# Two-layer diffusion trunk on one core: 22 value and gate tiles of layer 1 moved ahead of its attention, 16 of them in pairs of seven products

## The chip, the cores and the metric

The kernel runs on one core of one Trainium2 chip. The metric is the device time of one execution in microseconds (us). PE is TensorE (matmuls), PEld its weight load, DVE VectorE, ACT ScalarE, POOL GpSimd and SP SyncE; the two last issue most of the DMAs.

## What is computed

One inference step of a trunk with two layers. There are 640 tokens (128 of a prompt, 512 latent) of width D = 2048, all in fp32. Each layer is a norm with a learned shift and scale, one input projection, two attention-like branches, a gate, one output projection and a residual:

```python
hp = rms_norm(xp, norm_g[layer]) * (1.0 + sc_p) + sh_p      # hs likewise for the latent tokens
cq, ck, cv, cg, dq, dk, dv, dg = split_cols(h @ w_in, ODD_SPLIT)        # layer 1
o_c = rms_norm(o1 - lam * o2, c_on) * (1.0 - lam_init)      # C: two softmax maps a head, 4 heads, values 256 wide
y_c = o_c.transpose(0, 2, 1, 3).reshape(b, t, C_W) * jax.nn.silu(cg)
y_d = merge_heads(attend(q_d, dk_all, dv_all)) * jax.nn.silu(dg)        # D: 8 query heads on 2 key/value heads
out = jnp.concatenate([y_c, y_d], axis=-1) @ w_out
xp = xp + gt_p * out_p
```

Prompt tokens see prompt tokens alone; latent tokens see 256 cached keys and the 512 latent ones. The normalised keys and the values of the prompt are outputs too. Layer 1's input projection has 6656 columns: 52 tiles of 128 (cq 8, ck 8, cv 8, cg 8, dq 8, dk 2, dv 2, dg 8).

## The kernel before

Everything is kept transposed: 128 features on the partitions, 640 tokens along the free axis, in two halves of 320. An fp32 number is split in a high and a low part (`split`, L212: ACT copies the high part, DVE subtracts to get the low one), and each fp32 product is three matmuls: high by high, high by low, low by high (`proj_q`, L241; L248, L249, L250). h, the normalised input, stays in SBUF as 16 k-tiles, high and low. A **tile** of a projection is 128 columns: 2 halves x 16 k-tiles x 3 = 96 matmuls of 128x320, with weights loaded by SP in quarters of four k-tiles (`load_raw`, L224) and split ahead of use by ACT (`wh`, L213) and DVE (`wl`, L214).

`run_tiles` (L281) works through a list of jobs, each a column and a generator that post-processes the tile. The first three tiles are the **lead**: they go together, k-tile by k-tile, as `make_h` (in layer 1 `h1_maker`, L1217: per k-tile and token group one DVE scaling L1234, one ACT bias and rounding L1236, one DVE low part L1238) delivers h. Tile 4 needs an accumulator that lead tile 0 holds until its job has read it. Thereafter tiles go one by one; after each quarter `slot` (L273) advances the queue `prep` (post-processing of the last tile) and the queue `attn` by one step. Attention is thus a generator whose steps are interleaved by hand with the quarters of projection tiles; one step issues the scores of a block (`scores`, L681: L687 to L689), the softmax (`soft`, L652: maximum on DVE L654, scale L656 and exponential L661 on ACT, sum's reciprocal L667), transposes of an earlier block's weights (L675) and the products with the values. `k_gen` (L540) and `q_gen` (L587) normalise and rotate keys and queries; because there is one place for q0, q1, k0, k1 and v, they call `drain(attn)` before they overwrite it: whatever is left of the attention then runs at once.

In layer 1 each C head has the tiles ck, cq, ck, cq, cv, cv and the next head's two cg; the attention of a head (`diff_gen`, L1269) is queued after its second cv. D has dk, dv, then dq, dq and two dg per pair of query heads (`pair_gen`, L714). All 52 tiles run as plain tiles, 96 matmuls each.

`run_pairs` (L403) is another way to do two tiles at once, as a 2 x 2 block product with **seven products** in place of eight: 7 x 8 k-tiles x 3 = 168 matmuls for a pair in place of 192. The stationary operands are sums of weights (DVE, L434 and next), the moving ones are h's halves or forms of them: `forms` (L1019) makes, for each j of 8, three sums of h's quarter-blocks (320 columns each) and splits them into `T`, and a fourth one, `t1`, that `begin` (L1124) needs. The seven products are named Q1, N5, P6, Q2, P7, Q3, P4 in their order; the block sums overwrite parts of h (`half_of`) and use four places called `room`. Before the change only the output projections use it (`project_out`, L1072): three lead tiles and one more, then six pairs.

Between the layers the residual x is parked in DRAM (`xdram`) and comes back through `x1_back` (L1211), partly in the pairs' buffers w8, sx and T. The gated results y go to DRAM (`save_y`, L793, on POOL's queue) and are read back for the output projection by `y1_maker` (L1376).

Of the kernel before, what the change touches and what calls it, by code (L numbers as in the profile page):

```python
# [50 lines left out]
def trunk_kernel(ctx: ExitStack, tc: tile.TileContext, I: dict, O: dict):  # L51
# [164 lines left out]
    hs = {}  # L216

    def new_h(k):
        t = hpool.tile([P, 2, NT], F32R, tag=f"h{k}", name=f"h{k}")
        hs[k] = t[:, 0, :], t[:, 1, :]  # L220
        return hs[k]
# [39 lines left out]

    def advance(queue, n):
        for g in queue[:n]:
            if next(g, DONE) is DONE:
                queue.remove(g)
# [15 lines left out]
    def run_tiles(jobs, w_ap, make_h, fill=None, rate=0.0, ahead=None, order=(0, 1, 2, 3), before=None,  # L281
                  last=None, by_half=False, trans=[], grace=0, cut=None, summed=None, led=None, freed=None):
# [85 lines left out]
        for i in range(lead, len(jobs)):  # L368
# [34 lines left out]
    def run_pairs(cols, w_ap, mov, room, begin, done, tail):  # L403
# [60 lines left out]
        def after(p, name, ps):  # L464
# [7 lines left out]
            elif name == "Q2":  # L472
                V.tensor_add(q1, ps, q1)
                done(p, 0, 0, q1)
            elif name == "P7":
                A.copy(u3, ps)
                V.tensor_add(n5, u3, n5)
                done(p, 1, 1, n5)
            elif name == "Q3":
                V.tensor_add(u2, ps, u2)  # L480
                done(p, 0, 1, u2)
            else:
                done(p, 1, 0, ps)
# [56 lines left out]
    def k_gen(ap, pp, tag, src, gain, new_out):  # L540
# [33 lines left out]
        drain(attn)  # L574
# [9 lines left out]
        split(hi[:, CTX + NS:CTX + NT], lo[:, CTX + NS:CTX + NT], t)  # L584


    def q_gen(ap, pp, tag, gain, then=None, wait=True):  # L587
# [28 lines left out]
        drain(attn)  # L616
# [10 lines left out]
    def ctx_v(ap, src, hi, lo, w):  # L627
        raw = ap.tile([P, 2, w], F32, tag="ctxv", name="ctxv", bufs=1)
        nc.sync.dma_start(raw, src.rearrange("(c p) d -> p c d", p=P))
        split(hi[:, 0:2, :], lo[:, 0:2, :], raw)  # L630

    def v_gen(ap, pp, src, new_out, w=P, j=0, then=None):
        x = stage(ap, pp)
        yield
        if j == 0:
            drain(attn)
            st["v"] = tuple(ap.tile([P, 7, w], F32R, tag=t, name=t) for t in ("vh", "vl"))
            ctx_v(ap, src, *st["v"], w)
        hi, lo = st["v"]
        cols = slice(j * P, (j + 1) * P)  # L640
# [7 lines left out]
        if then:  # L648
            attn.append(then())
# [64 lines left out]
    def pair_gen(ap, width, k, banded, emit, done, sinks):  # L714

        v = st["v"]
# [25 lines left out]
        def score(u, j):  # L742
            segs, masks, lo, hi, _ = plan(u)
            q = st[f"q{j}"]
# [43 lines left out]
    xdram = [dram.tile([P, NT], F32, name=f"xd{k}") for k in range(KT)]  # L788

# [98 lines left out]
    def k_job(tag, src, gain, new_out):  # L888
        return lambda pp: k_gen(pools["cur"], pp, tag, src, gains[gain], new_out)
# [7 lines left out]
    def y_pair(i):  # L897
        t = pools["cur"].tile([P, 2, NT], F32, tag="y", name="y", bufs=2)
# [12 lines left out]
    def pair_then(width, kk, i, banded, gated):  # L911

        def then():
# [12 lines left out]
            sinks = [(nsink[:, j:j + 1], sink[:, j:j + 1]) if banded else () for j in (i, i + 1)]  # L926
            return pair_gen(pools["cur"], width, st[kk], banded, emit, done, sinks)
        return then

    def late_gate_job(i, load=False):  # L930
        def f(pp):
            ap = pools["cur"]
            if i < 8:
                drain(attn)
            if load and i % 2 == 0:
                y_pair(i)
                for k in (i, i + 1):
                    nc.sync.dma_start(y[k], ydram[k])
# [47 lines left out]
    for i in range(4):  # L986
# [5 lines left out]
        jobs.append((EV["q"] + (h + 1) * P, q_job("q1", "a_q_norm", pair_then(640, "k0", h, True, gated))))  # L992
# [25 lines left out]

    def forms():  # L1019
# [12 lines left out]
        for j in range(8):  # L1032
# [6 lines left out]
            x2, x3, x4 = (x[:, i * HALF:(i + 1) * HALF] for i in range(3))  # L1039
            V.tensor_sub(x3, b22, b12)  # L1040
            V.scalar_tensor_tensor(out=x2, in0=x3, scalar=-1.0, in1=b11, op0=ALU.mult, op1=ALU.subtract)
            V.scalar_tensor_tensor(out=x4, in0=x2, scalar=-1.0, in1=b21, op0=ALU.mult, op1=ALU.subtract)
            V.tensor_sub(d, b11, b12)
            t = big(f"T{j}", dtype=F32R).rearrange("p (s n) -> p s n", s=2)
            split(t[:, 0, :], t[:, 1, :], x)
            T.append(t)
            t1.append(d)
# [24 lines left out]
    def project_out(l, maker, finish, last, tail):  # L1072

        w = W_OUT[l]

        def job(n):
            def f(pp):
                res_load(l, n)
                for i in range(2):
                    res_sum(l, n, pp[i], CS[:1] if i == 0 else CS[1:])  # L1080
                for _ in range(1 + 2 * l):
                    yield
                finish(n)
            return f

        n0 = N_SINGLE[l]
        go_on = run_tiles([(n * P, job(n)) for n in range(3)], w, maker, order=(0, 2, 1, 3))


        quarters = [(n * P, qd) for n in range(3, n0) for qd in range(4)]  # L1090
# [10 lines left out]
        for n in range(3, n0):  # L1101
# [14 lines left out]
            prep.append(job(n)(pp))  # L1116
            advance(prep, 1)
# [12 lines left out]
        def done(p, t, c, src):  # L1130
            n, h = n0 + 2 * p + t, HX[c]
            res_sum(l, n, src, CS[1:] if h else CS[:1], nhgt if t else hgt)
            if n >= KT - 2:
                last(t, h)
            elif n in seen:
# [3 lines left out]
        run_pairs([(n * P, (n + 1) * P) for n in range(n0, KT, 2)], w,  # L1139
                  {"B11": half_of(0, 0), "T1": half_of(0, 1), "B21": half_of(8, 0), "B22": half_of(8, 1),  # L1140
                   "T2": form_of(0), "T3": form_of(1), "T4": form_of(2)}, room, begin, done, tail)
        drain(prep)


    make_y0 = y_maker(("q0h", "q0l", "q1h", "q1l"), NT)

    def y0_maker(k):
        if k < 4:
            return make_y0(k)
        if k == 8:  # L1150
            close("even")
            open_pool("mid")
            st["acc"] = pools["cur"].tile([P, NT], F32, name="acc")
            st["sq"] = pools["cur"].tile([P, NT], F32, name="sq")
# [51 lines left out]
    def x1_tail(name):  # L1206

        for k in (range(0, 4) if name == "Q2" else (4,)):
            x1_back(k, big("w8", bufs=4) if k < 4 else big("sx"))
# [6 lines left out]

    def h1_maker(k, hv):  # L1217
        if k == 0 and hv[0][0] == 0:
            for g in range(3):
                t = big(f"T{g}")  # L1220
                for i in range(3):
                    x1_back(5 + 3 * g + i, t, i)
            for i in (14, 15):
                x1[i] = st["xr", i]
            nc.sync.dma_start(tables, I["k_tables"])
        if len(hv) == 2 or hv[0][0] == 0:
            new_h(k)
            st["ht", k] = big(f"T{4 + k % 4}")[:, 0:NT]
        t = st["ht", k]
# [3 lines left out]
        for sl, c in toks:  # L1233
            V.scalar_tensor_tensor(out=t[:, sl], in0=x1[k][:, sl], scalar=gsc[1][:, k, c:c + 1],  # L1234
# [5 lines left out]
        if k == KT - 1:  # L1240
            close("mid")
            open_pool("odd")
            odd_start()


# [18 lines left out]
    def diff_then(h):  # L1264
        def then():
            return diff_gen(pools["cur"], h, gated.get(2 * h))
        return then

    def diff_gen(ap, h, gt):  # L1269

        v = st["v"]
        t = y_pair(2 * h) if gt is None else gt
# [4 lines left out]
        def score(u, m):  # L1277
            segs, masks, lo, hi, _ = blk_plan(u, False)
            n = hi - lo
            q = st[f"q{m}"]  # L1280
            s = scores(q, u, st[f"k{m}"], segs)
# [36 lines left out]
        def out(u):  # L1318
# [4 lines left out]
            if gt is None:  # L1323
# [21 lines left out]
    gated.clear()  # L1345
    jobs = []
    heads = (3, 0, 1, 2)
    for n, h in enumerate(heads):
        for m in range(2):
            jobs.append((OD["ck"] + (m * 4 + h) * P,  # L1350
# [119 lines left out]
```

## Time and profile before

| quantity | value |
|---|---|
| median of 3 runs | 2316.81 us (2316.61 to 2318.72) |
| profiled execution | 2320.95 us, its span 2319.2 us |
| mean granted TensorE clock in it | 0.997 |
| PE, DVE, ACT, POOL busy | 98%, 64%, 45%, 6% of the span |
| DMA | 321.91 MB, mean 139 GB/s |
| lead of layer 1 | 1141.5 to 1185.6 us |
| rest of layer 1's projection and attention | to about 2101 us |
| output projection 1 | to the end |

The profile is one execution's trace. A row of a group gives the line of the kernel, engine, operation, output and inputs by the program's names, the number of instructions, and behind the bar busy time, the mean duration in ns, and the idle time ahead of them with what ended it. A row of a timeline is start, duration, engine, line and names, in brackets the idle time before. Rows of stretches give start:end, and for each engine its busy time and count.

### The profile page before, as it was taken

The page shows a single profiled execution, that of the slowest core. Times are in us where ns is not written, and L with a number is a line of the kernel's source. Part 1 is how long each engine was busy: PE and PEld are TensorE (multiplying, and loading weights), DVE is VectorE, ACT ScalarE, POOL GpSimd, SP SyncE. Part 2 cuts the span into 40 slices and gives each one's busy share as a digit, 9 for nine tenths or more (in the row PEclk, how much of TensorE's full clock was granted, in tenths as well). Part 3 has the DMA queues.
Part 4 walks back from the last instruction along what each step waited for, and adds up shares of the span by engine and source line. Part 5 has one row for each costly group of instructions (what it writes and reads, how often), then busy time and mean ns, then how long its engine had stood idle before and what let it go on. Part 6 is the DMA issues. An engine that isn't in the chain of part 4 may idle for free.

```text
span 2319.2 us, 41035 instructions
## 1 busy us (share of the span) xinstructions
PE 2282.3 (98%) x16092; PEld 2209.7 (95%) x16092; DVE 1484.3 (64%) x2674; ACT 1035.5 (45%) x2186; POOL 131.4 (6%) x183
## 2 busy tenths in 40 slices
PE   7999999999999999999999999999999999999999
PEld 5889899999999999999999999999999999999999
DVE  4666978779779776887774445454454443457875
ACT  5325652443522222544554444444445554665443
POOL 1000000000000000000000000001000000000101
PEclk9999999999999999999999999999999999999999
DMA  9975546547367564954431221212222212127642
GB/s 320 294 249 160 158 121 214 151 132 218 115 211 222 179 190 129 291 155 127 162 98 58 79 75 55 87 58 77 75 68 65 62 47 81 48 74 263 189 137 61
DMA packets 371553, 321.91 MB, mean 139 GB/s; under 512 B 15762, under 2 KB 333680, under 8 KB 370848
## 3 DMA queue, kind: packets, MB, share of 16 engines
q1 hardware_dynamic: 363360, 288.92, 41.1%
q0 software_dynamic: 7280, 28.20, 3.4%
q8 instruction: 126, 2.06, 0.4%
q10 hardware_dynamic: 720, 2.16, 0.3%
q14 instruction: 67, 0.55, 0.1%
HBM read 290.79 MB, written 28.44 MB: 138 GB/s over the span
## 4 chain that ended last, share of the span: by engine, by line
PE 91%; DVE 3%; DMA 2%; ACT 2%; issue 1%; POOL 1%; SPq 0%; DVEq 0%; POOLq 0%; ACTq 0%
PE pa L248 11%; PE pb L248 10%; PE pb L249 10%; PE pa L249 10%; PE pb L250 10%; PE pa L250 10%; PE pq L499 4%; PE pq L498 4%; PE pq L497 4%; PE T L675 2%; PE S L687 1%; PE S L689 1%; PE S L688 1%; PE T L166 1%; PE T L526 1%; PE T L736 1%
## 5 line engine op out<-in xcount | busy, mean ns | idle before, releaser
L213 ACT ACTIVATE wh<-raw 128x512 fp32r<-128x512 f32 (+1 forms) x504 | 303.6, 604 | 736.2 <-PE pb L249 659.3
L214 DVE TENSOR_TENSOR wl<-raw,wh 128x512 fp32r<-128x512 f32 (+1 forms) x504 | 329.8, 655 | 388.5 <-ACT wh L213 356.2
L248 PE MATMUL pa<-h,wh 128*128 128x320 f32 x1728 | 551.3, 319 | 5.8 <-DVE sum L315 3.8
L249 PE MATMUL pa<-h,wh 128*128 128x320 f32 x1728 | 536.6, 311 | 0.5 <-DVE h L214 0.4
L250 PE MATMUL pa<-h,wl 128*128 128x320 f32 x1728 | 535.4, 310 | 0.0
L248 PE MATMUL pb<-h,wh 128*128 128x320 f32 x1728 | 535.3, 310 | 0.0
L250 PE MATMUL pb<-h,wl 128*128 128x320 f32 x1728 | 535.1, 310 | 0.0
L249 PE MATMUL pb<-h,wh 128*128 128x320 f32 x1728 | 535.0, 310 | 0.0
L248 PEld LDWEIGHTS pa<-h,wh 128*128 128x128 f32 x1728 | 325.4, 188 | 25.2 <-issue 15.5
L249 PEld LDWEIGHTS pa<-h,wh 128*128 128x128 f32 x1728 | 326.1, 189 | 4.5 <-issue 3.3
L250 PEld LDWEIGHTS pa<-h,wl 128*128 128x128 f32 x1728 | 325.1, 188 | 2.1 <-issue 2.1
L249 PEld LDWEIGHTS pb<-h,wh 128*128 128x128 f32 x1728 | 324.7, 188 | 0.9 <-issue 0.8
L248 PEld LDWEIGHTS pb<-h,wh 128*128 128x128 f32 x1728 | 324.6, 188 | 0.7 <-issue 0.4
L250 PEld LDWEIGHTS pb<-h,wl 128*128 128x128 f32 x1728 | 324.7, 188 | 0.4 <-issue 0.4
L191 DVE SCALAR_TENSOR_TENSOR acc<-adaw,sT,acc 128x1024 f32<-128x1024 f32 x240 | 300.0, 1278 | 0.0
L497 PE MATMUL pq<-h,wh 128*128 128x320 f32 x384 | 120.4, 314 | 1.0 <-ACT wh L213 1.0
L499 PE MATMUL pq<-h,wl 128*128 128x320 f32 x384 | 119.6, 311 | 0.8 <-DVE wl L214 0.8
L498 PE MATMUL pq<-h,wh 128*128 128x320 f32 x384 | 119.4, 311 | 0.0
L661 ACT ACTIVATE p<-S,nm,rq 128x768 f32<-128x768 f32 (+3 forms) x120 | 101.0, 842 | 23.1 <-DVE nm L658 20.0
L654 DVE TENSOR_REDUCE nm<-S 128x1 f32<-128x768 f32 (+3 forms) x120 | 91.9, 766 | 24.9 <-PE S L689 24.1
L213 ACT ACTIVATE pth<-T 128x512 fp32r<-128x512 f32 (+1 forms) x132 | 66.3, 532 | 51.5 <-PE T L675 51.0
L498 PE MATMUL pq<-T,wh 128*128 128x320 f32 x288 | 89.0, 309 | 0.0
(306 smaller groups left out, 3497.6 us busy)
## 6 DMA issues: line engine op xcount, KB each, us to landing
adaw<-in_ada_w SPq DMA_DIRECT2D x128, 512.0 KB, 4.3
raw<-in_od_w_in SPq DMA_DIRECT2D x208, 256.0 KB, 2.8
raw<-in_ev_w_in SPq DMA_DIRECT2D x176, 256.0 KB, 3.3
ada<-in_ada_w SPq DMA_DIRECT2D x32, 1024.0 KB, 8.2
yd<-y POOLq DMA_DIRECT2D x34, 320.0 KB, 3.0
yin<-yd SPq DMA_DIRECT2D x32, 320.0 KB, 4.3
w<-yd SPq DMA_DIRECT2D x32, 320.0 KB, 4.2
w<-in_ev_w_out SPq DMA_DIRECT2D x18, 512.0 KB, 4.9
```

What stands on the lines that cost most here:

```text
L191: V.scalar_tensor_tensor(out=acc[c], in0=w, scalar=sT[:, kt, c:c + 1], in1=acc[c], op0=ALU.mult, op1=ALU.add)
L213: A.activation(hi, x, AF.Copy)
L214: V.tensor_sub(lo, x, hi)
L248: PE.matmul(ps, wh[:, i, :], hi[:, sl], start=(j == js[0] if alone else (pos == 0 and j == 0)), stop=False)
L249: PE.matmul(ps, wh[:, i, :], lo[:, sl], start=False, stop=False)
L250: PE.matmul(ps, wl[:, i, :], hi[:, sl], start=False, stop=(j == js[1] - 1 if alone else (pos == 3 and j == 3)))
L497: PE.matmul(ps, wh[:, j, :], hi, start=(new and h == 0 and j == 0), stop=False, **kw)
L498: PE.matmul(ps, wh[:, j, :], lo, start=False, stop=False, **kw)
L499: PE.matmul(ps, wl[:, j, :], hi, start=False, stop=(h == 1 and j == 3), **kw)
L654: V.tensor_reduce(nm, s, axis=AX.X, op=ALU.max, negate=True)
L661: A.activation(p[:, 0:n], s, AF.Exp, scale=rsc, bias=nm, accum_out=l)
L675: PE.transpose(t[:, i * P:(i + 1) * P], p, ident)
```

## The change

The function `project` is what was common in `project_out`: a lead of three tiles, further singles, then pairs. Layer 1 now calls it first, with 22 tiles called FRONT: the gates 10 to 15 as singles (three of them the lead, while h is made), and then sixteen tiles in eight pairs: values 6, 7, gates 0, 1, values 0, 1, gates 2, 3, values 2, 3, gates 4, 5, values 4, 5, values 8, 9 (tiles 8 and up belong to D). Their results go to DRAM (`vdram`, `ydram`) on POOL's queue by way of a three-buffer place (`kept`, `keep_tile`). The pairs need T and t1 of layer 1's h: `forms1` is queued as an attention generator in the lead at k-tile 8 and advances when h of k-tile j+8 exists. `h1_maker` now scales x in place, since forms1 needs the scaled x again. The half of h that the pairs overwrite is saved to `hdram` k-tile by k-tile (eight DMAs on POOL's queue) and loaded back in the tail of the last pair's product P7 (eight more). The rotary tables are loaded after the pairs, not in the lead.

The other 30 tiles follow in a second `run_tiles` with `mid=True`, an extra attention step in the middle of the second quarter of each tile. Order: per C head cq, cq, ck, ck; for D dq, dq, dk, dq, dq per key head; at the end the gates 6 to 9. Queries have two sets of places ("a", "b"), used in turn. `release(tag)` advances only as long as an attention task that uses that place is queued, where `drain(attn)` emptied the queue. Values come back by `v_load` into one buffer (`vraw`); of a C head's two tiles the second is loaded after the first was transposed (`v_kept`). Gates that were done in FRONT are loaded into y's one buffer (`gated_y`; two before) ahead of the attention that multiplies by them; the late gates 6 to 9 load their y instead (`late_gate_job`).

```diff
+    def release(tag):
+        while any(tag in getattr(g, "tags", ()) for g in attn):
+            advance(attn, 1)
...
             for qd in range(4):
-                proj_q(pp, parts[t], qd, qd, HV[:1] if split_last else HV)
+                if mid and qd == 1:
+                    proj_q(pp, parts[t], qd, qd, HV[:1])
+                    advance(attn, 1)
+                    proj_q(pp, parts[t], qd, qd, HV[1:])
...
-        drain(attn)
+        release(tag)
...
+    def v_load(i):
+        t = pools["cur"].tile([P, NT], F32, tag="vraw", name="vraw", bufs=1)
+        nc.sync.dma_start(t, vdram[i])
+        return t
+
+    def v_kept(ap, first, raw, idx, new_out, then):
...
+        for j in range(len(idx)):
+            cols = slice(j * P, (j + 1) * P)
+            v_rows(ap, x, hi, lo, cols, new_out[:, cols])
+            if j + 1 < len(idx):
+                x = v_load(idx[j + 1])
+                yield
+        attn.append(then())
...
-            V.scalar_tensor_tensor(out=t[:, sl], in0=x1[k][:, sl], scalar=gsc[1][:, k, c:c + 1],
+            V.scalar_tensor_tensor(out=t[:, sl], in0=t[:, sl], scalar=gsc[1][:, k, c:c + 1],
...
+        if len(hv) == 2 or hv[0][0] == 1:
+            if k < 8:
+                nc.gpsimd.dma_start(hdram[k], ht[k][:, :, HV[HX[1]][1]])
+            made.add(k)
+        if k == 8:
+            attn.append(forms1())
+
+    def forms1():
...
+        for j, tag in enumerate((3, 4, 5, 6, 7, 1, 2, 0)):
+            while j + 8 not in made:
+                yield
+            for k in (j, j + 8):
+                for sl, c in TOKS:
+                    A.activation(x1[k][:, sl], x1[k][:, sl], AF.Identity, bias=mod[1][:, k, c:c + 1])
...
+            make_form(x, d, b11, b12, b21, b22, big(f"T{tag}", dtype=F32R))
+            yield
...
+    def front_job(n):
+        def f(pp):
+            kept(n)
+            for i, sl in HV:
+                gate_of(st["kept", n][:, sl], pp[i][:, 0:HALF])
+            keep_tile(n)
+        return f
...
+    def front_out(p, t, c, a, b):
+        n = N_FRONT + 2 * p + t
+        dst = st["kept", n][:, HV[HX[c]][1]]
+        if FRONT[n][0] == "g":
+            if b is not None:
+                V.tensor_add(b, a, b)
+            gate_of(dst, a if b is None else b, -1 if t else 1)
...
+    def front_tail(name):
+        if name == "P7":
+            for j in range(8):
+                nc.gpsimd.dma_start(ht[j][:, :, HV[HX[1]][1]], hdram[j])
+
+    project(I["od_w_in"][0], [front_col(*t) for t in FRONT], N_FRONT, h1_maker, front_job, front_begin, front_out,
+            front_tail, by_half=True)
+    nc.gpsimd.dma_start(tables, I["k_tables"])
...
+    def gated_y(i, late=False):
+        t = y_pair(i, 1)
+        if not late:
+            for k in (i, i + 1):
+                nc.sync.dma_start(y[k], ydram[k])
+        return t
...
+    run_tiles(jobs, I["od_w_in"][0], lambda k: odd_start() if k == 8 else None, mid=True)
```

More of the change, by code (lines that the diff above doesn't have):

```diff
@@ L1070, in form_of, with project @@
         return lambda j: (T[j][:, 0, i * HALF:(i + 1) * HALF], T[j][:, 1, i * HALF:(i + 1) * HALF])
[L1072 to L1090, printed above, removed]
+    def project(w, cols, n0, maker, job, begin, out, tail, by_half=False):
+        go_on = run_tiles([(cols[n], job(n)) for n in range(3)], w, maker, order=(0, 2, 1, 3), by_half=by_half)
+        quarters = [(cols[n], qd) for n in range(3, n0) for qd in range(4)]
         raws, parts = [], []
```

287 lines of the change are left out of this document (185 added, 102 removed).

## The prediction, on record before the changed kernel ran

> **What bounds the kernel now.** I read the page first (busy times, chain, DMA issues), then stretches of the trace, then single starts.
>
> ```profile
> span 2319.2 us, 41035 instructions
> PE 2282.3 (98%) x16092; PEld 2209.7 (95%) x16092; DVE 1484.3 (64%) x2674; ACT 1035.5 (45%) x2186; POOL 131.4 (6%) x183
> PE 91%; DVE 3%; DMA 2%; ACT 2%; issue 1%; POOL 1%; SPq 0%; DVEq 0%; POOLq 0%; ACTq 0%
> L498 PE MATMUL pq<-T,wh 128*128 128x320 f32 x288 | 89.0, 309 | 0.0
> ```
>
> TensorE is busy 98% of the span and 91% of the chain that ended last. A matmul removed from a stretch where PE never waits is therefore time removed. But 309 ns is not its price, because matmuls overlap. The price is the spacing of starts in a stretch that is nothing else. Columns below: stretch, its length, busy time (and count) of PE, PEld, DVE, ACT, POOL, then the granted clock, the DMA share and GB/s.
>
> ```profile
> 950.00:1000.00 50.00, 47.64 (x306) 46.25 (x306) 43.69 (x76) 24.79 (x42) 2.16 (x4) 0.97 0.87 263
> 1050.00:1100.00 50.00, 50.00 (x343) 50.00 (x343) 39.12 (x62) 23.44 (x41) 2.16 (x4) 1.00 0.45 133
> 1138.30:1176.80 38.50, 37.06 (x240) 36.24 (x240) 36.12 (x82) 23.67 (x46) 1.10 (x1) 0.96 0.44 147
> 1185.56:1216.00 30.44, 28.66 (x201) 26.43 (x199) 18.73 (x38) 18.61 (x52) 4.87 (x5) 1.00 0.31 90
> 1981.00:2034.00 53.00, 53.00 (x385) 52.24 (x383) 25.41 (x48) 33.65 (x68) 0.00 (x0) 1.00 0.16 46
> 2063.00:2101.00 38.00, 37.98 (x266) 35.54 (x265) 23.23 (x43) 26.82 (x55) 1.48 (x3) 1.00 0.23 72
> ```
>
> The second row is pairs of seven products in layer 0's output projection: 50.00/343 = 145.8 ns per matmul. PE never waits there, with DVE at 78% and ACT at 47%. The first row holds the start of those pairs, the third the lead of layer 1 (its first three tiles, while h is made). There **DVE is busy 36.1 of 38.5 us**: PE is nearly bound by DVE already.
>
> **The change part by part.**
>
> *Removed.* A pair of tiles by seven products is 7 x 8 x 3 = 168 matmuls against 2 x 96 = 192 before. Eight pairs remove 192 matmuls: 192 x 0.1458 = **-28.0 us**. The instruction order of the two kernels bears the count out (192 fewer on TensorE); the second row shows that pairs can run at full rate.
>
> *The lead of layer 1.* New work stands here: forms1 makes, for each of eight j, the sums that the pairs multiply with. As soon as h for k-tile j+8 exists, the form is appended, so it competes with h itself. Prices, from the same work in layer 0's output projection (rows: busy us, mean ns, idle before):
>
> ```profile
> L1040 DVE TENSOR_TENSOR sx<-w,w 128x320 f32<-128x320 f32 x8 | 3.9, 484 | 0.0
> L1042 DVE SCALAR_TENSOR_TENSOR sx<-sx,w 128x320 f32<-128x320 f32 x8 | 3.9, 485 | 0.0
> L1041 DVE SCALAR_TENSOR_TENSOR sx<-sx,w 128x320 f32<-128x320 f32 x8 | 3.9, 486 | 0.0
> L1043 DVE TENSOR_TENSOR tables<-w 128x320 f32<-128x320 f32 x4 | 1.9, 485 | 0.0
> L214 DVE TENSOR_TENSOR T<-sx,T 128x960 fp32r<-128x960 f32 x8 | 9.3, 1157 | 1.0 <-ACT T L213 1.0
> 1174.12 1.01 DVE L1238 SCALAR_TENSOR_TENSOR h<-T,mod,h 128x512 fp32r<-128x512 f32 x2
> 1175.04 1.01 DVE L1234 SCALAR_TENSOR_TENSOR T<-xr,gsc,sf 128x512 f32<-128x512 f32 x2
> 1175.97 0.68 DVE L214 TENSOR_TENSOR wl<-raw,wh 128x512 fp32r<-128x512 f32 x1
> 1176.58 1.01 DVE L1238 SCALAR_TENSOR_TENSOR h<-T,mod,h 128x512 fp32r<-128x512 f32 x2
> 1185.56 0.31 PE L248 MATMUL pa<-h,wh 128*128 128x320 f32 x1
> ```
>
> One form is 4 x 0.485 + 1.157 = 3.10 us of DVE; the timeline rows show that each instruction starts about 0.08 us before the last ended (1174.12 + 1.01 = 1175.13, next start 1175.04), so five of them take 2.7 us. In the order of DVE's instructions four whole forms stand ahead of the last low half of h: 10.8 us. That half ended at 1176.58 + 1.01 = 1177.59. DVE had 38.50 - 36.12 = 2.4 us to spare, so it now ends between 1186.0 and 1188.4. The gate that empties lead tile 0's accumulator then stands behind six more 0.485 us form steps, one 1.16 us split, three weight splits of about 0.65 and one more form step: about 6 us less overlaps, with 0.5 for the gate itself. Tile 4 needs that accumulator, and so starts at 1192.3 to 1194.7 where it started at 1185.56. I take 1193.9: **+8.3 us** (5, if DVE finds the idle time and the order is kinder, to 12, if nothing overlaps). The four later forms lie beside three single tiles, 3 x 96 x 0.146 = 42 us of PE; they are hidden. ACT carries four 320-to-640-wide steps and a 1 us split per form on 24 of 38.5 us: not the bound.
>
> *The clock.* A lead whose PE starves can lose clock as well:
>
> ```profile
> 153.74 0.61 PE L248 MATMUL pa<-h,wh 128*128 128x320 f32 x1 [2.55 <-DVE sum L315]
> 153.80:157.30 3.50, 3.50 (x14) 3.50 (x15) 1.02 (x4) 0.25 (x1) 0.00 (x0) 0.53 0.32 95
> 987.48 0.41 PE L497 MATMUL pq<-h,wh 128*128 128x320 f32 x1 [0.99 <-ACT wh L213]
> 988.70 0.41 PE L499 MATMUL pq<-h,wl 128*128 128x320 f32 x1 [0.66 <-DVE wl L214]
> 990.24 0.47 PE L499 MATMUL pq<-h,wl 128*128 128x320 f32 x1
> ```
>
> After a gap of 2.55 us the granted clock was 0.53 for 3.5 us and 14 matmuls ran where 24 would have: 10 x 0.146 = 1.5 us lost. After gaps of 0.99 and 0.66 us, two microseconds apart, matmuls were again at the slow pace (0.47 against 0.31 us). The starved lead will hold gaps of that kind: I take one such dip, **+1.5 us** (0 to 3: two). The Trainium skill, "TensorE: Matmul & The Clock Gate", section "HAM oscillation — how this bites in real kernels", gives as the rule that only PE idle gaps above some 3.4 us bring the slow clock; by that rule this term would be zero and the sum 1.5 us lower. The rows above speak against it (2.55 us sufficed, and 0.99 with 0.66), so the term stays.
>
> *Start of the pairs.* The same two gaps at 987-989 came from weights that landed late:
>
> ```profile
> 986.01 1.29 DVE L434 TENSOR_TENSOR sx<-w,raw 128x512 f32<-128x512 f32 x2 [1.88 <-DMA w<-in_ev_w_out]
> ```
>
> They cost 1.65 us and a dip of 1.5, 3.2 in all. Here two more singles than in layer 0's projection stand ahead (3 after the lead, not 1), so loads start earlier: **+0.5** (0 to 3.7).
>
> *From the pairs to the other 30 tiles.* New waits: half 0 of h for k below 8, overwritten by the pairs' sums, comes back by eight 320 KB loads on POOL's queue, issued when the last pair's product P7 has ended and two are left. Nearest price:
>
> ```profile
> yd<-y POOLq DMA_DIRECT2D x34, 320.0 KB, 3.0
> w<-xd SPq DMA_DIRECT2D x4, 320.0 KB, 3.0
> y<-yd SPq DMA_DIRECT2D x2, 320.0 KB, 3.6
> w<-yd SPq DMA_DIRECT2D x32, 320.0 KB, 4.2
> ```
>
> Eight issues at about half a microsecond and 3 us to land are about 7 us; two products (2 x 24 x 0.146 = 7.0 us) cover them. Behind them on POOL stands only the load of the rotary tables, needed much later. **+1** (0 to 6, the whole if the cover is gone). Kept tiles are saved from POOL, which has 131 us of work in 2319, and the eight saves of h go the same way during the lead: 0.
>
> *Attention.* It now has 30 tiles to hide behind, not 52, and five steps per tile instead of four (mid=True). A step needs its scores, then this chain:
>
> ```profile
> 1249.61 0.34 PE L689 MATMUL S<-k0h,q0l 128*128 128x384 f32 x1
> 1250.04 0.95 DVE L654 TENSOR_REDUCE nm<-S 128x1 f32<-128x768 f32 x1
> 1251.17 0.29 ACT L656 ACTIVATE nm<-nm,rq 128x1 f32<-128x1 f32 x1
> 1251.50 0.99 ACT L661 ACTIVATE p<-S,nm,rq 128x768 f32<-128x768 f32 x1
> 1253.96 0.34 PE L687 MATMUL S<-k1h,q1h 128*128 128x384 f32 x1
> ```
>
> From the end of the scores (1249.95) to the end of the exponential (1252.49) are 2.5 to 2.7 us; the next scores start 4.0 us after. With a step at every half quarter (12 matmuls, 1.75 us, plus the step's own matmuls) spacings of 2.3 to 2.9 us come about: just the length of the chain. The stretch 2063-2101 above already runs so (one step per half quarter): 266/37.98 = 7.00 matmuls per us against 385/53 = 7.26 in 1981-2034. At the latter rate 266 take 36.6 us, so 1.4 us were lost there. There are eight such attention groups, seven of them new to it; only one in five of their steps is denser for the mid steps, but the chains now meet more weight splits and loads. I take 0.9 each for seven, less the 1.4 that is no longer paid at the end: **+5** (0 to 14: 2 each).
>
> *Values come back from DRAM.* One buffer (vraw): the second tile of a C head is loaded only when the first is transposed. A 320 KB load takes 3.0 to 3.6 us (rows above); 20 matmuls, 2.9 us, stand between. About 0.5 for each of four heads: **+2** (0 to 4).
>
> *Output projection 1.* The last tile's gate (9) now ends its y last, and y9 is needed as the second k-group: gate, save (3.0) and load back (4.2) are about as long as the 10.6 us until then: **+0.5** (0 to 3). Tables loaded later, x1 scaled in place, gate tiles loaded instead of computed in the window: same work elsewhere, 0. The waits of the second lead (1185-1216: 30.44 - 28.66 = 1.8 us) move with it, 0.
>
> Sum: -28.0 + 8.3 + 1.5 + 0.5 + 1 + 5 + 2 + 0.5 = **-9.2 us**. The profiled execution took 2320.95 (span 2319.2), so 2311.8; that execution lies 4.14 above the median 2316.81, so I predict **2307.6**.
>
> **The rivals.**
>
> *Dense attention eats the gain (no change).* At 2 us per group (+14, not +5) the sum is -0.2: 2316.6. For it: the stretch 2063-2101. Against it: that stretch has a step in every half quarter, the new one only every fifth.
>
> *Slower: the chain of a step outlasts its spacing.* Scores, maximum, exponential and weight splits go through DVE and ACT in order. If weight splits (0.68 each) slip between, a step needs 3.1 us where its spacing is 2.3 to 2.9, and PE, in order too, stops at the next scores. With some 96 steps, five in eight at the short spacing: 60 x 0.4 = 24 us, 19 more than I took: 2326.6. It decides from 0.32 us per short step (60 x 0.32 = 19.2, past 2321.4). Against it: ACT is at 27/38 and DVE at 23/38 in 2063-2101, and PE is busy 37.98 of 38.00 there.
>
> *All new waits hidden.* DVE's forms slip into idle time and steps are spaced evenly: -28 + 5 (lead) + 3: 2296.8. Against it: the full DVE of the lead.
>
> *It does not do what it says.* If pairs were no faster than tiles (DVE-bound by their sums), the 28.0 would be missing and the other terms left: 2316.8 + 18.8 = 2335.6. The second row speaks against it, DVE being 78% there, and the sums into the residual that end a pair there give way to gates of a like number of 320-wide steps.
>
> **How the numbers follow.** Forecast (2302 to 2312) 0.55; no change 0.15; slower 0.13; all hidden 0.15; no saving 0.02. Faster than 2312.2 (0.2%, about what a measurement of this kernel can tell from no change): 0.70. Within 0.2%: 0.15. Slower than 2321.4: 0.15. Bounds of the terms, all low: -28 + 5, less 1.4: 2292; all high: far past 2330; two such ends at once are unlikely. The range **2296 to 2320** leaves out the slower cases and the tail of the all-hidden one, some 0.2.
>
> **What would show it.** Right: tile 4 of layer 1 starts 8 us later against the end of the norm; the pairs run at 343 matmuls in 50 us with no idle; small gaps ahead of scores in the dense tiles; 192 fewer matmuls. Wrong: PE idle for microseconds at each group of steps (slower), waits of PE on loads of h, vraw or y, a lead that ends as before (all hidden), DVE near 100% in the pairs (no saving).

## The result, and the profile after

The change made the kernel slower by a quarter of a percent: 2324.11 us against 2318.40 (medians of 13 runs each), ratio 1.0025 (95% interval 1.0015 to 1.0035). The forecast was 2307.6, range 2296 to 2320.

The page of the changed kernel first: PE is busy for 12.5 us less than before, and yet the span is 7.4 us longer. (These are the two profiled executions, 7.5 us apart; the medians are 5.7 us apart.) The 43% of the chain row can't be set against the 91% of before: the row's shares add up to 59%, since the chain could be followed back only to 974 us. Of the chain behind that time PE has about three quarters, where it had 95% before the change: more of it now runs through other engines.

```profile
span 2326.6 us, 41104 instructions
PE 2269.8 (98%) x15900; PEld 2182.8 (94%) x15900; DVE 1589.4 (68%) x2831; ACT 1094.9 (47%) x2304; POOL 159.9 (7%) x224
PE 43%; DVE 6%; ACT 4%; issue 3%; DMA 2%; POOL 1%; SPq 0%; POOLq 0%; DVEq 0%; ACTq 0%
```

To see where, cut the trace at the first and last matmuls of the stages (stretches with the columns named in the prediction). Before: lead of layer 1, the rest up to the start of output projection 1, the pairs of output projection 1.

```profile
1141.51:1185.56 44.05, 44.05 (x291) 43.26 (x290) 37.13 (x83) 26.49 (x53) 0.00 (x0) 0.98 0.42 130
1185.56:2101.00 915.44, 913.07 (x6380) 895.03 (x6379) 429.48 (x835) 458.72 (x1029) 64.64 (x83) 1.00 0.23 69
2158.56:2314.00 155.44, 155.44 (x1073) 154.41 (x1071) 107.42 (x169) 68.30 (x134) 16.33 (x26) 1.00 0.40 118
```

After: lead, the eight pairs, the other 30 tiles with the attention, the pairs of output projection 1.

```profile
1142.71:1194.73 52.02, 45.79 (x291) 43.50 (x290) 49.84 (x107) 42.59 (x86) 4.74 (x7) 0.97 0.59 172
1237.07:1434.03 196.96, 196.96 (x1346) 196.96 (x1345) 128.40 (x186) 87.04 (x161) 14.88 (x25) 1.00 0.38 114
1434.03:2104.00 669.97, 655.59 (x4555) 626.33 (x4554) 369.86 (x741) 398.87 (x926) 69.94 (x86) 1.00 0.27 81
2162.68:2322.00 159.32, 156.98 (x1073) 155.86 (x1071) 107.91 (x168) 68.86 (x134) 16.47 (x26) 0.99 0.40 115
```

| stage | before | after | difference |
|---|---|---|---|
| up to layer 1's lead (code unchanged) | 1141.5 | 1142.7 | +1.2 |
| lead | 44.05 | 52.02 | +8.0 |
| tile 4 to the first pair of output projection 1 (the "third stage" below) | 973.0 | 42.3 + 197.0 + 728.7 = 968.0 | -5.0 |
| first to last matmul of that projection's pairs | 155.2 | 159.0 | +3.8 |

The eight pairs took 197.0 us with PE never idle. As sixteen plain tiles of 96 matmuls at 0.1466 us they would have taken 225.2: the 28 us were saved. But the third stage is 5 us shorter, not 28: **23 us went lost in the 30 tiles with attention**. The lead cost 8 more and output projection 1 nearly 4. PE idles for 669.97 - 655.59 = 14.4 us of the 30 tiles' stretch, against 2.4 in the longer one before; since a matmul's row is 0.31 us long while starts are 0.147 apart, about 0.16 us of each wait is hidden behind the matmul before it.

What PE waited for, before and then after, in the stretch 1186 to 2101 (waits in all, times, longest):

```profile
PE T L526 <- DVE m L571: 0.8, 2, 0.4
PE T L526 <- DVE k0l L214: 0.8, 1, 0.8
PE T L603 <- DVE k1l L214: 0.2, 1, 0.2
```

```profile
PE T L1454 <- DVE on L1448: 5.7, 12, 0.9
PE T L539 <- DVE m L584: 2.2, 2, 1.4
PE T L1439 <- DVE ptl L214: 1.9, 4, 0.7
PE S L722 <- ACT p L696: 1.3, 6, 0.3
PE pa L248 <- DVE kept L1333: 1.1, 1, 1.1
PE T L771 <- DVE ptl L214: 0.9, 1, 0.9
PE T L618 <- DVE vp L652: 0.5, 2, 0.3
PE T L539 <- DMA vraw<-vd: 0.2, 1, 0.2
```

L1454 are the transposes of a C head's finished block (`on`), L1439 and L771 products with the values, L722 scores. Counted by starts (how far each start lies beyond the usual distance to the one before), the third stage holds about 8 us more ahead of the output transposes than before, 8 to 9 more in the scores and some 4 more in the products with the values, depending on the distance that is taken as usual: 20 to 21 of the 23.

The output transposes show how it comes about. From a block's products with the values a chain leads over scale and square (ScalarE), a power (GpSimd) and a scaling (VectorE) to the transposes. Before the change 24 tile matmuls stand between products and transposes in 16 of the 20 C blocks, and 39 in the others. Last product, scaling and transposes of one of them:

```profile
1257.05 0.28 PE L1306 MATMUL T<-vh,ptl 128*128 128x256 f32 x1
1259.93 0.48 DVE L1315 SCALAR_TENSOR_TENSOR on<-on,rn,con 128x256 f32<-128x256 f32 x1 [0.69 <-POOL rn L1314]
1260.69 0.38 PE L1321 MATMUL T<-ident,on 128*128 128x128 f32 x2
```

The chain takes 3.1 us from the products' end (1257.33 to 1260.41), the tile matmuls cover it, and PE waits for none of these 16. After the change the second block of each head has only 12 tile matmuls there, and its transposes wait for 0.84 to 0.88 us:

```profile
1635.48 0.28 PE L1439 MATMUL T<-vh,ptl 128*128 128x256 f32 x1
1638.70 0.48 DVE L1448 SCALAR_TENSOR_TENSOR on<-on,rn,con 128x256 f32<-128x256 f32 x1 [0.74 <-POOL rn L1447]
1639.24 0.44 PE L1454 MATMUL T<-ident,on 128*128 128x128 f32 x2 [0.85 <-DVE on L1448]
```

In the first block there are still 24, but the chain takes 3.6 us, and the wait is 0.2. The last block has 19 to 23 where it had 39, and waits for 0.3 to 0.45. These twelve waits are the 5.7 us of the row above.

### The profile page after: what moved, and what is told of

Read it like the earlier page. It is cut to its first block, busy times and chain, and to the rows that moved or that the text cites. A ratio compares the mean times of both kernels' runs of the same rounds, so it can differ in the third digit from the quotient of the medians.

```text
span 2326.6 us, 41104 instructions
## 1 busy us (share of the span) xinstructions
PE 2269.8 (98%) x15900; PEld 2182.8 (94%) x15900; DVE 1589.4 (68%) x2831; ACT 1094.9 (47%) x2304; POOL 159.9 (7%) x224
## 4 chain that ended last, share of the span: by engine, by line
PE 43%; DVE 6%; ACT 4%; issue 3%; DMA 2%; POOL 1%; SPq 0%; POOLq 0%; DVEq 0%; ACTq 0%
PE pq L512 7%; PE pq L511 7%; PE pq L510 7%; PE pb L249 3%; PE pb L248 3%; PE pb L250 3%; PE pa L248 2%; PE pa L249 2%; PE pa L250 2%; PE T L710 1%; PE S L722 1%; ACT qsw L610 1%; ACT p L696 1%; PE T L539 1%; PE S L724 1%
## 5 line engine op out<-in xcount | busy, mean ns | idle before, releaser
L248 PE MATMUL pa<-h,wh 128*128 128x320 f32 x1456 | 464.4, 320 | 10.3 <-ACT h L1286 3.8
L249 PE MATMUL pa<-h,wh 128*128 128x320 f32 x1456 | 453.6, 312 | 1.6 <-DVE h L1288 0.7
L248 PE MATMUL pb<-h,wh 128*128 128x320 f32 x1456 | 452.3, 311 | 0.5 <-ACT h L1286 0.5
L250 PE MATMUL pa<-h,wl 128*128 128x320 f32 x1456 | 452.5, 311 | 0.0
L250 PE MATMUL pb<-h,wl 128*128 128x320 f32 x1456 | 451.6, 310 | 0.0
L249 PE MATMUL pb<-h,wh 128*128 128x320 f32 x1456 | 450.8, 310 | 0.0
L248 PEld LDWEIGHTS pa<-h,wh 128*128 128x128 f32 x1456 | 274.9, 189 | 26.2 <-issue 12.0
L249 PEld LDWEIGHTS pa<-h,wh 128*128 128x128 f32 x1456 | 275.1, 189 | 6.9 <-issue 3.3
L248 PEld LDWEIGHTS pb<-h,wh 128*128 128x128 f32 x1456 | 273.6, 188 | 1.8 <-ACT h L1286 1.0
L249 PEld LDWEIGHTS pb<-h,wh 128*128 128x128 f32 x1456 | 273.8, 188 | 0.8 <-issue 0.8
L510 PE MATMUL pq<-h,wh 128*128 128x320 f32 x640 | 199.4, 312 | 2.4 <-ACT wh L213 2.4
L512 PE MATMUL pq<-h,wl 128*128 128x320 f32 x640 | 198.7, 310 | 1.7 <-DVE wl L214 1.7
L511 PE MATMUL pq<-h,wh 128*128 128x320 f32 x640 | 198.2, 310 | 0.0
L512 PE MATMUL pq<-T,wl 128*128 128x320 f32 x480 | 147.7, 308 | 0.2 <-DVE wl L214 0.2
L511 PE MATMUL pq<-T,wh 128*128 128x320 f32 x480 | 147.9, 308 | 0.0
L510 PE MATMUL pq<-T,wh 128*128 128x320 f32 x480 | 147.7, 308 | 0.1
```

What stands on the lines that cost most here:

```text
L248: PE.matmul(ps, wh[:, i, :], hi[:, sl], start=(j == js[0] if alone else (pos == 0 and j == 0)), stop=False)
L249: PE.matmul(ps, wh[:, i, :], lo[:, sl], start=False, stop=False)
L250: PE.matmul(ps, wl[:, i, :], hi[:, sl], start=False, stop=(j == js[1] - 1 if alone else (pos == 3 and j == 3)))
L510: PE.matmul(ps, wh[:, j, :], hi, start=(new and h == 0 and j == 0), stop=False, **kw)
L511: PE.matmul(ps, wh[:, j, :], lo, start=False, stop=False, **kw)
L512: PE.matmul(ps, wl[:, j, :], hi, start=False, stop=(h == 1 and j == 3), **kw)
```

## The experiments

The theory after the trace: three separate causes. Forms in the lead fill VectorE; the attention steps, some of them half a quarter apart, follow each other faster than the latency chains behind them; and these chains are longer, since ScalarE and VectorE now have the post-processing of query and key tiles in between. The rivals say that the extra step relieves, that the waits only move, or that something else in the lead is slow. All times are medians; the kernel before stood at 2318 to 2319 beside them.

**no_mid**, the extra step away:

```diff
-    run_tiles(jobs, I["od_w_in"][0], lambda k: odd_start() if k == 8 else None, mid=True)
+    run_tiles(jobs, I["od_w_in"][0], lambda k: odd_start() if k == 8 else None)
```

> The changed kernel without the extra attention step in the middle of each tile's second quarter (mid=False). In the changed kernel's trace the stretch of the 30 tiles lost about 23 us more to PE waits than the same work before; steps that follow each other by 12 tile matmuls hold 7.9 us of it. Theory M (the extra step makes the steps too dense): without it that stretch gets 6 to 8 us shorter, time 2316 to 2318 against 2324. Rival R (the extra step relieves: 13 steps of a C head's attention have about 10 quarters until its keys are overwritten, so without it some 3 steps a head run in one block with nothing between): the stretch gets 5 to 12 us longer, 2329 to 2336.

Measured: 2312.81, ratio to before 0.9973 (0.9964 to 0.9983), 11.3 us below the change. Rival R falls: 70 of the 80 steps with scores stand 24 tile matmuls behind the one before. Theory M has the sign right and the size wrong. The excess in the scores fell by 5 to 6 us, but by the trace the third stage lost 3.4 us in all, and output projection 1's pairs another 4.4, which nobody had expected; the other 3.5 us between the medians were not traced to a stage. At the output transposes the wait of the second block is gone, but the first block now waits for 0.74 us and the last, with only 14 to 17 tile matmuls in between, for 0.60.

**out_late**, output transposes one step later:

```diff
         for u in range(7):
-            if u >= 2:
-                out(u - 2)
             if u < 5:
                 score(u, 0)
...
             if u < 5:
                 score(u, 1)
+            if u >= 2:
+                out(u - 2)
```

> The changed kernel with one thing moved: in the C heads the transposes of a finished block's output are issued after the second scores of a unit instead of ahead of the first ones, one attention step later. Theory C (a latency chain: values' products, scale and square on ScalarE, power on GpSimd, scaling on VectorE, then the transposes; PE waited 8.3 us more ahead of these transposes than before the change): these waits nearly vanish and the time falls by 6 to 8 us, to 2316 to 2318. Rival D (VectorE and ScalarE are simply too full in these tiles, the transposes are only the place where it shows): the waits move to scores and value products, and the time falls by less than 2 us.

Measured: 2319.68, ratio 1.0009 (1.0001 to 1.0018): 4.4 us better than the change, 3.6 of it in the third stage. Between the two. PE's waits show both halves: those on `on` fell from 5.7 to 1.6 us (the last block of each head), others rose.

```profile
PE T L1437 <- DVE ptl L214: 2.8, 3, 0.9
PE T L539 <- DVE m L584: 2.2, 2, 1.4
PE S L722 <- ACT p L696: 2.1, 10, 0.3
PE T L1454 <- DVE on L1448: 1.6, 4, 0.4
```

**forms_late**, the forms queued when the lead is over (`led`, called in `project`), not at k-tile 8:

```diff
-        if k == 8:
-            attn.append(forms1())
...
         go_on()
+        if led:
+            attn.append(led())
```

> The changed kernel with the forms for the pairs made after the lead, beside the three single tiles, instead of within the lead. Theory L (the lead is 8.0 us longer because VectorE makes four forms ahead of the last low halves of h): lead of layer 1 back to 43 to 45 us from 51.1, the pairs start as before, time 6 to 8 us less, 2316 to 2318. Rival S (scaling x in place and the saves of h to DRAM lengthen the lead): lead stays within 1 us of 51, time the same. Rival P (the forms then come too late): the pairs' start moves out by several us and the gain is lost there.

Measured: 2315.90, ratio 0.9991 (0.9982 to 1.0000). Theory L holds: the lead is as long as before the change, and the pairs start 42.7 us behind tile 4 as they did (42.3). The work is the same; only its place is new.

```profile
1137.25:1180.63 43.38, 43.38 (x290) 43.15 (x290) 40.39 (x89) 37.55 (x81) 5.29 (x8) 0.98 0.64 185
```

**out_forms**, the last two together:

> Both moves together: output transposes one step later, and the forms after the lead. If both causes are independent (theories C and L), the time falls by the sum, 12 to 16 us, to 2308 to 2312, some 0.3 to 0.4% faster than before the change. If the two gains share a cause (a full VectorE), the sum is clearly less than the two alone.

Measured: 2314.59, ratio 0.9983 (0.9973 to 0.9993): 9.5 of 12.6 us. The trace says why it is no full sum: the third stage is 2.0 us shorter than the change's, not 3.6, and the lead 44.5, not 43.4. PE waited in neither lead; the granted clock was 0.95 in the longer one and 0.98 in the other, so that 1.1 us is not the work of the moves. Neither reading of the expectation is clearly borne out.

**nomid_forms**, no extra step and the forms late:

> The changed kernel without the extra step in the second quarter and with the forms made after the lead. Alone the first gave 2312.8 and the second 2315.9, from 2324.1. If the two causes are independent (the lead's VectorE work; the density of attention steps 200 us later) the gains add: 2304 to 2306, some 0.6% under the kernel before. If the first gain was partly the same microseconds (the stall where the pairs of output projection 1 start, which went with the first and stayed with the second), still 2304 to 2306, with that stall gone; if the stall comes back, 2308 to 2310.

Measured: 2305.20, ratio 0.9945 (0.9933 to 0.9957). The gains add (11.3 + 8.2 = 19.5, measured 18.9). With these two edits the change is 0.55% faster than the kernel before. Its third stage, from tile 4, is 961.8 us, still 17 more than the 945 that 28 us of savings would leave.

**nomid_forms_out**, and the output transposes later:

> As the kernel beside it, and the output transposes of the C heads one attention step later. In the run without the extra step PE's excess ahead of these transposes is still 10.2 us against 2.2 before the change. Theory C (a chain of 3.1 to 4.7 us that one step's distance does not hide): 4 to 6 us less than the kernel beside it, 2299 to 2301. Rival D (full ScalarE and VectorE, waits move on): under 2 us less, 2303 to 2305.

Measured: 2306.66, ratio 0.9950 (0.9938 to 0.9961): no gain, and the rival D is right here. The waits moved to other instructions of PE's queue: counted by starts, the excess ahead of the output transposes fell by some 3 us, while it rose by 1 to 2 in the scores and by 2 ahead of the transposes of the weights. The third stage is 0.3 us shorter.

**no_rope**, the rotation of layer 1's queries left out of the changed kernel:

```diff
-        for d in range(4):
-            A.copy(sw[32 * d:32 * d + 32, :], x[32 * (d ^ 1):32 * (d ^ 1) + 32, 0:NS])
-        V.tensor_mul(sw, sw, sinT)
...
-        V.tensor_add(m, m, sw)
```

> The changed kernel with the rotation of layer 1's queries left out (the latent tokens' queries are scaled by the cosine table only): 16 query tiles lose four ScalarE copies of 0.62 us and two VectorE steps of 0.69 each, 39.5 us of ScalarE and 22 of VectorE; PE's work is the same. Crowding theory (the attention of a head now runs beside the post-processing of query and key tiles, and since ScalarE and VectorE work in order, the short chains that PE waits for stand behind it): the stretch of the 30 tiles gets 6 to 12 us shorter, time 2312 to 2318. Rival, distance (steps follow each other too closely, whatever else the engines do): under 2 us, 2322 to 2325.

Measured: 2322.22, ratio 1.0024 (1.0014 to 1.0033): 1.9 us. Counted by starts, the waits at output transposes and scores shrank by 2 us. The third stage as a whole is 2.2 us longer than the change's all the same, because in this trace the lead of output projection 1, its last part, waited 2.7 us for its input, and 3.4 us at a granted clock of 0.50 followed; that projection's pairs took 2.4 us less. Crowding is not what costs most while some steps stand half a quarter apart.

**one_q**, one set of query places:

> The changed kernel with one set of query places in place of two: a head's attention must then be over before the next head's first queries are written, about one tile after it starts, so some 8 of 13 steps run in a block with no tile matmuls between. A step alone needs its chain of 2.5 us (scores to exponential) against 1.1 us of scores: 8 heads x 8 steps x about 1 us: 50 to 80 us longer, 2370 to 2400, if the second set carries the arrangement. If it carries little: 2322 to 2330.

Measured: 2324.37, ratio 1.0026 (1.0015 to 1.0037): the same as the change. My expectation was far off: the steps spread differently (5 to 18 tile matmuls between most of them where it was 12 to 24), and hardly any ran bare. By the time, the second set of places is worth nothing measurable here. The trace has two opposite differences behind that: the third stage is 4.6 us longer than the change's, output projection 1's pairs 3.1 shorter.

**nomid_forms_norope**, the rotation left out where the close steps are gone:

> The version without the extra step and with the forms after the lead (2305.2), with the rotation of layer 1's queries left out (cosine table only). In its trace the two long waits of each C head ahead of the output transposes (1.1 and 0.8 us) have ScalarE start the scaling 1.3 and 0.7 us late, behind the rotation's copies. Crowding theory, now that the close steps are gone: these waits fall, 1 us or more per C head and some at the scores, 3 to 6 us in all: 2299 to 2302. Rival (the attention stretch is slower for its own order of steps and not for its neighbours): under 1.5 us, 2304 to 2305.

Measured: 2302.52, ratio 0.9930 (0.9916 to 0.9943): 2.7 us, just under the expected 3; in the trace 3.4 us of the third stage. Crowding is real but small. Of the two waits of each C head that the expectation blamed on the copies, only the first, 0.74 us ahead of the first block's transposes, went with them. The second, 0.60 ahead of the last block's, stayed: its scaling had started 0.04 us behind the products, and the 14 to 17 tile matmuls there are too few to cover 3.0 us. The timeline of the version with rotation shows the first. ScalarE, around the chain of one block: its products with the values ended at 1610.47, and the scaling of `on` starts at 1611.78, behind a copy of the rotation (0.62) and an exponential (0.99); another copy stands between the scaling and the square.

```profile
1610.15 0.62 ACT L610 COPY qsw<-qx 32x512 f32<-32x512 f32 x1
1610.80 0.99 ACT L696 ACTIVATE p<-S,nm,rq1b 128x768 f32<-128x768 f32 x1
1611.69 0.19 ACT L696 ACTIVATION_READ_ACCUMULATOR p<-S,nm,rq1b 128x1 f32 x1
1611.78 0.46 ACT L1441 ACTIVATE on<-T,rl 128x256 f32<-128x256 f32 x1
1612.27 0.62 ACT L610 COPY qsw<-qx 32x512 f32<-32x512 f32 x1
1612.91 0.42 ACT L1444 ACTIVATE junk<-on 128x256 f32<-128x256 f32 x1
```

Then GpSimd's power, VectorE's scaling and the transposes, which wait:

```profile
1613.75 0.87 POOL L1447 TENSOR_TENSOR rn<-ssq,half 128x1 f32<-128x1 f32 x1 [14.69 <-DVE ssq L1445]
```

```profile
1615.29 0.41 PE L1454 MATMUL T<-ident,on 128*128 128x128 f32 x2 [0.74 <-DVE on L1448]
```

From the products' end to the transposes are 4.8 us. Before the change the same chain took 3.1 us and its transposes came 3.35 us behind the products: it was hidden by 0.3 us. That was the whole margin in three of a head's five blocks.

**rope_pool**, the copies on GpSimd, with nothing left out:

```diff
-            A.copy(sw[32 * d:32 * d + 32, :], x[32 * (d ^ 1):32 * (d ^ 1) + 32, 0:NS])
+            f = G.tensor_copy if tag[-1] in "ab" else A.copy
+            f(sw[32 * d:32 * d + 32, :], x[32 * (d ^ 1):32 * (d ^ 1) + 32, 0:NS])
```

> The version without the extra step and with the forms after the lead (2305.2), with the four copies of the rotation of each layer 1 query tile done by GpSimd instead of ScalarE; nothing is left out. Leaving the whole rotation out gave 2302.5. If ScalarE's copies are what delays the scaling ahead of the output transposes and GpSimd (busy 7% of the span) takes them without delay, the time falls by 1.5 to 2.7 us, to 2302.5 to 2304. Rival: GpSimd is slower at copies than ScalarE's 0.62 us each and the queries, and the powers that it works out for the outputs, come late: 2306 to 2312.

Measured: 2306.16, ratio 0.9943 (0.9929 to 0.9956): no gain, as the rival said, and in the trace a third stage 2.3 us longer. The waits on `on` halved, as without the rotation, but a wait on the values' post-processing and one on the queries' sums came up instead; GpSimd's copies take 0.72 us.

```profile
PE T L619 <- DVE vp L653: 3.6, 4, 1.1
PE T L1455 <- DVE on L1449: 2.4, 4, 0.6
PE T L539 <- DVE m L584: 2.2, 2, 1.4
PE T L1455 <- ACT qs L622: 1.9, 4, 0.5
```

**five_pairs**, gates 0 to 5 as plain tiles between the C heads:

```diff
+        if n < 3:
+            for i in (2 * n, 2 * n + 1):
+                jobs.append((front_col("g", i), light_gate(i)))
```

> The version without the extra step and with the forms after the lead (2305.2), with gates 0 to 5 taken out of the pairs and put back as plain tiles behind each C head's keys, two per head as before the change; five pairs are left. That gives back 3 x 3.5 = 10.5 us of matmuls. Dilution theory (the waits come because a head's steps now run only beside query and key tiles; beside light gate tiles they were hidden): the C heads' excess falls by 9 to 12 us and the time is 2304 to 2307, no gain from the last three pairs. Rival (tiles beside attention make no difference): 2315 to 2316, the three pairs are worth their full 10.5.

Measured: 2313.53, ratio 0.9978 (0.9969 to 0.9986): 8.3 us slower than with eight pairs, between both theories. By the traces, from tile 4 to output projection 1's pairs it is 967.2 against 961.8: of the 10.5 us given back, 5.1 returned as waits that went. By the medians it is only 2.2. So tiles without heavy post-processing beside the attention hide between a fifth and a half of what the three pairs gain; these runs don't settle it closer.

## Why the prediction was wrong, point by point

- *Pairs, -28.0*: right. 197.0 us for eight pairs, 28.2 less than plain tiles, PE never idle, VectorE at 65%.
- *Lead, +8.3*: right, 8.0. The last low half of h ended 9.8 us later against the lead's start than before, six form steps, three weight splits, a form split and one more step stood ahead of the gate, and tile 4 started right behind it. The two rows are the first form step behind h and that gate (ended 1194.67; tile 4 started at 1194.73):

```profile
1188.45 0.50 DVE L1057 TENSOR_TENSOR sx<-T,acc 128x320 f32<-128x320 f32 x1
...
1194.19 0.48 DVE L1333 SCALAR_TENSOR_TENSOR kept<-kept,pa 128x320 f32<-128x320 f32 x1
```

 forms_late took the whole term away.
- *A dip of the clock, +1.5*: it did not come in this trace, and that was luck. The clock of the lead was 0.97 (0.98 before) because of its first 2.9 us; from 1145.6 on it was 1.00, though PE stood still for up to 1.64 us. Five traces have this lead with the same waits. In no_mid and no_rope it took 52.2 and 52.4 us; in one_q and out_late the wait of 1.64 us was followed by 3.4 us at half clock, and the lead took 54.1 and 54.2. So the term was 0 in three traces and 2 us in two. The row is the lead of one_q:

```profile
1136.43:1190.54 54.11, 47.87 (x290) 45.65 (x289) 49.98 (x107) 42.55 (x86) 4.73 (x7) 0.93 0.58 169
```

- *Start of the pairs, +0.5, and from the pairs to the other tiles, +1*: both 0. The first plain matmul follows the last pair's at the usual distance; the eight loads of h were hidden, at 5.5 us to land instead of the 3.0 that I took.

```profile
1433.88 0.31 PE L512 MATMUL pq<-T,wl 128*128 128x320 f32 x1
1434.03 0.31 PE L248 MATMUL pb<-h,wh 128*128 128x320 f32 x1
```

- *Values from DRAM, +2*: 0.2 us. The load lands in 2.9 us.
- *Attention, +5 (0 to 14)*: **this is the step that failed.** It measured 23, with the term before it. I priced one chain, scores to exponential, and set its 2.5 to 2.7 us against the spacing of steps. That chain alone cost 8 to 9 us, by the excess in the scores, so even the priced part was too low. There are two more chains in a step, and I put both at nothing: products with the values to output transposes (3.1 us, over three engines behind PE), which cost about 8, and the exponential to the values' products, about 4. A transpose that is late holds up PE, as the rows with 0.85 us show, so each of the three counts. The first of the two had a margin of 0.3 us before, which the rows of its chain would have told.
 The working has two wrong readings here. In the stretch at 2063-2101, from which I took 1.4 us a group, only 6 to 11 tile matmuls stand between steps, less than the half quarter (12) that I wrote; and it belongs to a D group, which has no output norm and so no chain through it. And I called one step in five denser in one place, and five in eight in another. In the trace three of the nine distances between a C head's steps are 12 tile matmuls, two are 16 to 20 and four are 24, where before the change all were 24.
 Shown by runs: the extra step costs 3.4 us here; the rotation's crowding 3.4, once the extra step is gone; tiles without heavy post-processing between the heads would hide 2 to 5. These need not add up, and some 8 of the 17 us that remain without the extra step were not traced to one cause. What several runs do show of the rest is that single moves shift it: out_late with nomid_forms, and rope_pool, each took one wait away and gave another.
- *Output projection 1, +0.5 (0 to 3)*: 3.8. The pairs' first weights came late: two waits, 1.44 and 0.90 us, and a clock of 0.99 over the stage, the two-gap start that I had priced at 3.2 us, but for the front's pairs. It stood in the runs out_late, forms_late and out_forms too (158.5 to 159.5 us) and was gone without the extra step (154.6 to 155.6 in no_mid and nomid_forms). one_q and no_rope, with the extra step, had less of it (155.9 and 156.6), but their third stage was 4.6 and 2.2 us longer than the change's. In SyncE's queue the changed kernel loads the last three y tiles 17 us behind the first five (rows below), since weight loads that wait for buffers stand between; without the extra step all eight go first. That this order is the cause is argued from the traces and wasn't tried alone; one_q and no_rope load their last three y tiles late as well (15 to 18 us behind), and waited only 0.9 and 1.5 us there, so the order can't be all of it.

```profile
2091.52 6.74 SPq L1552 DMA_DIRECT2D yin<-yd  x5
2098.87 10.08 SPq L226 DMA_DIRECT2D raw<-in_od_w_out  x4
2109.11 1.34 SPq L1552 DMA_DIRECT2D yin<-yd  x3
```

- The slower rival (2326.6) had the right sign and the right kind of mechanism, a chain of a step that outlasts its spacing, but only one of the three chains: the scores hold 8 to 9 us where it put 24. That its time comes near 2324.1 is in part luck. I gave it 0.13. I weighed it against DVE's and ACT's shares of busy time, which say nothing about latency.

Against the sum: -28.2 + 8.0 + 23 + 3.8 + 1.2 (drift ahead of the change) = +7.8; the last matmul starts 7.9 us later. That is between the two profiled executions; the medians differ by 5.7.

## What to carry to other kernels

Taking filler tiles away from a hand-interleaved attention takes cover from *every* latency chain in a step; list each chain that the matmul queue meets (scores, products, output), with its length and its margin, before you price the new spacing. New work that feeds a later stage doesn't belong in a stretch where VectorE is already full (36.1 of 38.5 us in the lead): behind it the same forms cost nothing here. When a moved wait comes back elsewhere with the same size, stop moving waits and change the spacing.

## What the runs showed of the hardware that was not expected

Whether a gap of PE is followed by a stretch at half clock differed from trace to trace for the same code: the lead's gap of 1.64 us, with others of 0.47, 0.54 and 0.72 us, was followed by none in three traces (the changed kernel, no_mid, no_rope) and by 3.4 us at a granted clock of 0.50 in two (one_q, out_late), some 2 us of time. The gaps of 0.99 and 0.66 us before the change (they end 1.2 us apart) were followed by one as well, so neither kind of gap is a sure sign. Eight 320 KB saves and eight loads on GpSimd's queue took 5.8 and 5.5 us to land (medians) where single ones took 3.0. The part of layer 0 whose code is the same in all kernels ended between 1135.0 and 1142.7 us in the traces, so a single trace tells a stage's length but not a total to better than some microseconds.
